# Delta rule on one Trainium2 core: diagonal squares of 16 rows inverted by back substitution on VectorE in place of three doubling levels

## The chip, the cores and the metric

The kernel runs on 1 core of one Trainium2 chip. The metric is device time in microseconds of one execution. TensorE (PE in the rows, with PEld for its weight loads), VectorE (DVE), ScalarE (ACT) and GpSimd (POOL) each run their own instructions in a fixed order; SyncE (SP) issues the DMAs of the kernel before.

## The reference, cut to what matters

Two layers of a hybrid decoder over 256 tokens and 1024 channels. Each layer projects the hidden state, mixes the tokens in three ways (gated DeltaNet, Mamba-2 SSD, MLA attention), merges the three and runs a feed-forward part: dense in layer 0, 8 experts in layer 1. The change lies in the DeltaNet:

```
ia  = eye(C) + where(strict_lower, beta[:, None] * kk * decay, 0)
rhs = concat([v * beta, k * (beta * exp(G))])
sol = triangular_solve(ia, rhs, lower=True, unit_diagonal=True)
...
v_new = u - w @ state
o     = q_dec @ state + qk @ v_new
```

`kk` holds the products of all keys, `decay` their decays, and `ia` is unit lower triangular, so the solve is a product with its inverse. There are 4 heads of 128 channels.

## The kernel before, in words

The kernel works in 2 chunks of 128 tokens (index `t`, `NT` = 2), with the 4 heads side by side in 512 columns of one tile. In `gdn()` it makes, for each `t`, the strictly lower part `N[t]` (line 1062: VectorE reads the product of the keys from PSUM) and then the inverse of identity plus `N[t]`, held in `Sm[t]`.

The inverse is built by doubling. Lines 1075 to 1078 write the inverse of the squares of 2 rows (a product with a mask and a subtraction from the identity, both of 512 columns on VectorE). The loop `lv` from 1 to 6 (line 1087) then doubles the side of the inverted squares from 2 to 128 rows. One level is, for both `t`: 8 products `N` by `Tm` on TensorE (line 1098, tile `smt`), a masked copy into `M1` on VectorE (line 1101, 256 columns; GpSimd clears the rest of `M1`, line 1100), 8 products `M1` by `Sm` (line 1108), a subtraction into `Sm` on VectorE (line 1109) and, up to level 5, 8 transposes of `Sm` (`turn`, line 1073) that ScalarE copies into `Tm`. All products with `Sm`, `Tm`, `N` and `M1` are in plain f32; a trace shows each of them as two passes through TensorE, and a transpose as one.

What fills TensorE meanwhile: every weight comes as a raw f32 tile of 1 MB by DMA, ScalarE rounds it into `whi` (line 170) and VectorE takes the remainder `wlo` (line 172), 128x1024 at a time through a ring of four, and each product is done as three products of rounded halves. `ada_step` (line 199) spreads the conditioning vectors over the same time, one VectorE instruction of 128x1024 after another.

The order of the work: `gdn()`, `ssd()` and a list of fill steps (three convolutions, gates, branch products) are generators. `weave` (line 521) takes one step of `gdn`, one of `ssd` and one of the fill in turn, and `yield` marks where a step ends. Within what that order allows, the framework's scheduler sets the order on each engine when the program is built. Each engine then works strictly in that order.

Of the kernel before, what the change touches and what calls it, by code (L numbers as in the profile page):

```python
# [10 lines left out]
F32 = mybir.dt.float32  # L11
# [3 lines left out]
AF = mybir.ActivationFunctionType  # L15
# [4 lines left out]
P = 128  # L20
# [41 lines left out]
def trunk_kernel(ctx, tc, a, out, dbg=None):  # L62
# [32 lines left out]
    def mm(o, l, r, start, stop):  # L95
        return T.matmul(o, l, r, start=start, stop=stop, skip_group_check=True)  # L96
# [88 lines left out]
    def smtile():  # L185
        return pp.tile([P, 512], F32, name="smt", tag="sm", bufs=3)
# [346 lines left out]
    def mixer(l, after=None):  # L533

        with tc.tile_pool(name=f"mx{l}", bufs=1, reuse_waits="tile") as mp, \
# [3 lines left out]
            def wg(name, dt=F32):  # L539
                return mp.tile([P, 512], dt, name=name, tag="w2k", bufs=16)  # L540
# [469 lines left out]
            def gdn():  # L1010
# [52 lines left out]
                                               op0=OP.mult, op1=OP.mult)  # L1063
                yield

                Sm = [wg("Sm") for _ in range(NT)]
                Tm = [wg("Tm") for _ in range(NT)]
                idb = ident.unsqueeze(1).to_broadcast([P, 4, P])

                def turn(t):  # L1070
                    ps = trtile()
                    for h in range(4):
                        T.transpose(ps[:, hsl[h]], Sm[t][:, hsl[h]], ident)  # L1073
                    A.activation(Tm[t], ps, AF.Copy)
                for t in range(NT):
                    tmp = wg("tmp")
                    V.tensor_mul(h4(tmp), h4(N[t]), cst[:, C_LT0:C_LT0 + P].unsqueeze(1).to_broadcast([P, 4, P]))
                    V.tensor_sub(h4(Sm[t]), idb, h4(tmp))
                qr = raw_rows(0)
                yield  # L1080
                qn = normed(0, *qr)
                yield
                for t in range(NT):
                    turn(t)
                qT = [turned(qn[t]) for t in range(NT)]
                yield
                for lv in range(1, 7):
                    b = 1 << lv
                    lo_ = lambda x: x.rearrange("p (m two b) -> p m two b", two=2, b=b)[:, :, 1]
                    up_ = lambda x: x.rearrange("p (m two b) -> p m two b", two=2, b=b)[:, :, 0]  # L1090
                    v = lambda x: x.rearrange("p (m b) -> p m b", b=b)
                    mk = cst[:, C_LVL + 64 * lv - 64:C_LVL + 64 * lv].rearrange("p (m b) -> p m b", b=b)
                    mk = mk.unsqueeze(1).to_broadcast([P, 4, 64 // b, b])
                    M1s = []
                    for t in range(NT):
                        ps = smtile()
                        for h in range(4):
                            mm(ps[:, h * 64:(h + 1) * 64], N[t][:, hsl[h]], up_(Tm[t][:, hsl[h]]), True, True)
                        M1 = wg("M1")
                        G.memset(lo_(M1), 0.0)  # L1100
                        V.tensor_mul(M1.rearrange("p (h m two b) -> p h m two b", h=4, two=2, b=b)[:, :, :, 0],
                                     ps[:, :256].rearrange("p (h m b) -> p h m b", h=4, b=b), mk)
                        M1s.append(M1)
                    yield
                    for t in range(NT):
                        ps2 = smtile()
                        for h in range(4):
                            mm(ps2[:, h * 64:(h + 1) * 64], M1s[t][:, hsl[h]], lo_(Sm[t][:, hsl[h]]), True, True)
                        V.tensor_sub(lo_(Sm[t]), lo_(Sm[t]), v(ps2[:, :256]))
                    yield  # L1110
                    if lv < 6:
                        for t in range(NT):
                            turn(t)
                    if lv == 2:
                        for t in range(NT):
                            At.append(wg("At"))
                            ps = smtile()
                            for h in range(4):
                                mm(ps[:, hsl[h]], kT[t][:, hsl[h]], qT[t][:, hsl[h]], True, True)
                            V.tensor_mul(At[t], ps, E[t])  # L1120
                    if lv == 3:
                        while fill.has("v"):
                            yield
                        for t in range(NT):
                            psv = trtile()
                            for h in range(4):
                                T.transpose(psv[:, hsl[h]], vc[h][:, t * P:(t + 1) * P], ident)
                            vt.append(wg("vt"))
                            A.activation(vt[t], psv, AF.Copy)
                    if lv < 6:  # L1130
                        yield
                og = []
# [663 lines left out]
```

## Time and profile before

| | us |
|---|---|
| median of 3 runs | 1904.64 (1902.97 to 1906.03) |
| the profiled execution | 1905.8 |
| its span in the trace | 1904.0 |
| TensorE busy | 1847.7 (97%) |
| VectorE busy | 1598.7 (84%) |
| ScalarE busy | 1230.9 (65%) |
| GpSimd busy | 41.5 (2%) |

The token mixing of layer 0 runs until about 322 us, the dense feed-forward part until about 560, the mixing of layer 1 until about 860, and the experts take the rest. `N` is written at 149 us in layer 0 and at 647 us in layer 1; the six levels that follow end at 244 us in layer 0. A busy share is the time that an engine spends inside instructions. For TensorE it says little on how near to its peak it is, since a matmul that is pipelined behind another counts with its whole length. The distance from one start to the next tells what an instruction costs; for TensorE it is read from the weight loads.

### The profile page before, as it was taken

The page shows a single profiled execution, that of the slowest core. Times are in us where ns is not written, and L with a number is a line of the kernel's source. Part 1 is how long each engine was busy: PE and PEld are TensorE (multiplying, and loading weights), DVE is VectorE, ACT ScalarE, POOL GpSimd, SP SyncE. Part 2 cuts the span into 40 slices and gives each one's busy share as a digit, 9 for nine tenths or more (in the row PEclk, how much of TensorE's full clock was granted, in tenths as well). Part 3 has the DMA queues.
Part 4 walks back from the last instruction along what each step waited for, and adds up shares of the span by engine and source line. Part 5 has one row for each costly group of instructions (what it writes and reads, how often), then busy time and mean ns, then how long its engine had stood idle before and what let it go on. Part 6 is the DMA issues. An engine that isn't in the chain of part 4 may idle for free.

```text
span 1904.0 us, 25647 instructions
## 1 busy us (share of the span) xinstructions
PE 1847.7 (97%) x9490; PEld 1548.6 (81%) x9490; DVE 1598.7 (84%) x2313; ACT 1230.9 (65%) x1599; POOL 41.5 (2%) x61
## 2 busy tenths in 40 slices
PE   8989999999999999999999999999999999999996
PEld 6889888788879898888888777878878888788785
DVE  7988786876578987667999889998898999899997
ACT  4655445544455644446777787777777777777775
POOL 0000100000000000000000000000000000000001
PEclk9999999999999999999999999999999999999998
DMA  9463545676545555558899989999889999899892
GB/s 364 175 213 125 199 177 202 241 290 238 205 169 199 198 185 193 176 200 329 334 356 343 354 320 361 343 365 355 339 333 356 351 358 368 311 354 381 332 353 91
DMA packets 75016, 530.19 MB, mean 278 GB/s; under 512 B 8578, under 2 KB 8962, under 8 KB 12548
## 3 DMA queue, kind: packets, MB, share of 16 engines
q1 hardware_dynamic: 74884, 528.49, 73.6%
q8 instruction: 76, 1.25, 0.3%
q14 instruction: 56, 0.46, 0.1%
HBM read 527.41 MB, written 1.05 MB: 278 GB/s over the span
## 4 chain that ended last, share of the span: by engine, by line
PE 84%; DVE 8%; ACT 4%; DMA 2%; issue 2%; ACTq 0%; DVEq 0%; SPq 0%
PE mmt L96 74%; PE smt L96 5%; DVE wlo L172 2%; DMA raw<-in_w_in_dram 2%; PE sst L96 2%; PE trt L1566 1%; DVE raw L199 1%; ACT whi L170 1%; DVE cv L588 1%; ACT sg L1527 1%; PE trt L258 0%; PE trt L1073 0%; PE trt L96 0%; DMA raw<-in_ffn_w_up_dram 0%; ACT htmp L289 0%
## 5 line engine op out<-in xcount | busy, mean ns | idle before, releaser
L172 DVE TENSOR_TENSOR wlo<-raw,whi 128x1024 fp32r<-128x1024 f32 (+1 forms) x874 | 1041.9, 1221 | 151.7 <-ACT whi L170 131.6
L170 ACT ACTIVATE whi<-raw 128x1024 fp32r<-128x1024 f32 (+1 forms) x874 | 907.8, 1059 | 316.4 <-PE mmt L96 263.4
L96 PE MATMUL mmt<-whi,xx 128*128 128x512 f32 x1792 | 578.9, 397 | 0.0
L96 PEld LDWEIGHTS mmt<-whi,xx 128*128 128x128 f32 x1792 | 337.4, 188 | 74.9
L96 PE MATMUL mmt<-wlo,xx 128*128 128x512 f32 x896 | 357.6, 399 | 4.9 <-DVE wlo L172 4.9
L96 PE MATMUL mmt<-whi,act 128*128 128x512 f32 x896 | 281.0, 391 | 1.2 <-ACT whi L170 1.2
L96 PEld LDWEIGHTS mmt<-wlo,xx 128*128 128x128 f32 x896 | 168.8, 188 | 52.1 <-DVE wlo L172 16.5
L96 PEld LDWEIGHTS mmt<-whi,act 128*128 128x128 f32 x896 | 167.4, 188 | 36.4 <-ACT whi L170 2.5
L96 PE MATMUL mmt<-whi,hh 128*128 128x512 f32 (+2 forms) x480 | 183.9, 389 | 4.8 <-ACT hh L292 2.0
L96 PE MATMUL mmt<-wlo,hh 128*128 128x512 f32 (+2 forms) x480 | 180.9, 382 | 1.0 <-DVE wlo L172 1.0
L96 PE MATMUL mmt<-whi,hl 128*128 128x512 f32 (+2 forms) x480 | 180.8, 382 | 0.5 <-DVE hl L293 0.5
L96 PE MATMUL mmt<-wlo,act 128*128 128x512 f32 x448 | 175.2, 391 | 1.8 <-DVE wlo L172 1.6
L199 DVE CUSTOM_DVE_ANT_0 raw<-raw,sc_b,pv 128x1024 f32<-128x1024 f32 x96 | 121.7, 1281 | 7.9 <-DMA raw<-in_w_ada_gate_dram 4.7
L96 PEld LDWEIGHTS mmt<-whi,hh 128*128 128x128 f32 x480 | 90.7, 189 | 22.8 <-ACT hh L292 2.6
L96 PEld LDWEIGHTS mmt<-whi,hl 128*128 128x128 f32 x480 | 90.6, 189 | 18.0 <-DVE hl L293 1.0
L96 PEld LDWEIGHTS mmt<-wlo,hh 128*128 128x128 f32 x480 | 90.6, 189 | 17.4 <-DVE wlo L172 1.6
L96 PEld LDWEIGHTS mmt<-wlo,act 128*128 128x128 f32 x448 | 84.1, 188 | 22.3 <-DVE wlo L172 4.4
L96 PE MATMUL mmt<-hh,wlo 128*128 128x256 f32 x320 | 92.9, 292 | 4.4 <-DVE wlo L172 4.4
L96 PE MATMUL mmt<-hh,whi 128*128 128x256 f32 x320 | 93.4, 293 | 1.5 <-ACT whi L170 1.5
L96 PE MATMUL mmt<-hl,whi 128*128 128x256 f32 x320 | 92.1, 289 | 0.0
L1549 ACT ACTIVATE act<-trt 128x512 fp32r<-128x512 f32 x56 | 33.1, 591 | 72.0 <-PE trt L1566 72.0
L96 PEld LDWEIGHTS mmt<-hh,wlo 128*128 128x128 f32 x320 | 61.9, 194 | 6.0 <-DVE wlo L172 5.8
(422 smaller groups left out, 2209.6 us busy)
## 6 DMA issues: line engine op xcount, KB each, us to landing
raw<-in_moe_w_gate_dram SPq DMA_DIRECT2D x112, 1024.0 KB, 5.9
raw<-in_moe_w_up_dram SPq DMA_DIRECT2D x112, 1024.0 KB, 6.4
raw<-in_moe_w_down_dram SPq DMA_DIRECT2D x112, 1024.0 KB, 6.6
raw<-in_w_in_dram SPq DMA_DIRECT2D x50, 1024.0 KB, 4.9
raw<-in_w_ada_pair_dram SPq DMA_DIRECT2D x32, 1024.0 KB, 5.5
raw<-in_w_ada_gate_dram SPq DMA_DIRECT2D x16, 1024.0 KB, 4.9
raw<-in_ffn_w_down_dram SPq DMA_DIRECT2D x11, 1024.0 KB, 4.8
raw<-in_ffn_w_gate_dram SPq DMA_DIRECT2D x10, 1024.0 KB, 4.9
```

Of the source, the lines that this page charges most:

```text
L96: return T.matmul(o, l, r, start=start, stop=stop, skip_group_check=True)
L170: last["hi"] = A.activation(hi[:, :m], r, AF.Copy)
L172: last["lo"] = V.tensor_sub(lo[:, :m], r, hi[:, :m].bitcast(F32))
L199: last["ada"] = V.tensor_tensor_reduce(r, r, sc_b, 1.0, pv[l][:, PP_BADA + i:PP_BADA + i + 1], OP.mult, OP.add, modc[l][:, i:i + 1])
L588: V.scalar_tensor_tensor(cv[:, s:], o[:, :S - s], tapw(3 - s), cv[:, s:], op0=OP.mult, op1=OP.add)
L1527: A.activation(tmp[:, o], ps[:, o], AF.Identity, scale=sc, bias=sh)
L1549: return trace(*args, **kw)
L1566: last["tr"] = T.transpose(ps[:, b * P:(b + 1) * P], sg[:, b * P:(b + 1) * P], ident)
```

## The change

The levels 1 to 3 and the start with squares of 2 rows go. In their place the 64 diagonal squares of 16 rows (8 squares in each chunk, 2 chunks, 4 heads) are inverted at once, each in one partition of VectorE:

- GpSimd writes both `N[t]` (256 KB each) to a buffer in HBM, `blk_in`, and reads the 64 squares back into `B`, one partition each, by four DMAs of 16 squares, in pieces of 64 bytes. It clears `X` and sets its diagonal to one.
- VectorE changes the sign of `B` (64x256) and does 15 pairs of a product of n by n and a sum over rows of n, n from 1 to 15. Each pair needs the one ahead of it.
- GpSimd writes the 64 inverted squares into a second buffer, `blk_out`, by four DMAs, and loads both `Sm[t]` (256 KB each) from it. What lies outside the squares in `blk_out` is zero; it is cleared once, in layer 0 behind the first products, by a memset on GpSimd and three DMAs of 525 KB together.
- The products `At` and the transposes `vt`, which stood in levels 2 and 3, come behind the back substitution, then `turn`, then the levels 4 to 6 as before.

```diff
+BROW = 16 * 512 + 16
...
+    blk_in = dp.tile([NT * 8, BROW], F32, name="blk_in")
+    blk_out = dp.tile([NT * 8, BROW], F32, name="blk_out")
+    blk_rows = lambda x, t: x[8 * t:8 * t + 8].rearrange("m c -> (m c)")[:P * 512].rearrange("(p c) -> p c", c=512)
+    blk_diag = lambda x, h: x[:, :16 * 512].rearrange("m (j c) -> m j c", j=16)[:, :, h * P:h * P + 16]
...
+                zero = wg("zero")
+                G.memset(zero, 0.0)
+                to = blk_out.rearrange("m c -> (m c)").rearrange("(p c) -> p c", p=P)
+                w = NT * 8 * BROW // P
+                for c in range(0, w, 512):
+                    n = min(512, w - c)
+                    nc.gpsimd.dma_start(to[:, c:c + n], zero[:, :n])
...
+                blk = lambda name: wm(name)[:64, :256].rearrange("p (j i) -> p j i", j=16)
+                B, X = blk("B"), blk("X")
+                for t in range(NT):
+                    nc.gpsimd.dma_start(blk_rows(blk_in, t), N[t])
+                for h in range(4):
+                    nc.gpsimd.dma_start(B[16 * h:16 * h + 16], blk_diag(blk_in, h))
+                x_flat = X.rearrange("p j i -> p (j i)")
+                G.memset(x_flat, 0.0)
+                G.memset(x_flat[:, ::17], 1.0)
...
-                for t in range(NT):
-                    tmp = wg("tmp")
-                    V.tensor_mul(h4(tmp), h4(N[t]), cst[:, C_LT0:C_LT0 + P].unsqueeze(1).to_broadcast([P, 4, P]))
-                    V.tensor_sub(h4(Sm[t]), idb, h4(tmp))
                 qr = raw_rows(0)
                 yield
                 qn = normed(0, *qr)
                 yield
+                V.tensor_scalar(B, B, -1.0, None, op0=OP.mult)
+                prod = wm("prod")
+                for j in range(14, -1, -1):
+                    n = 15 - j
+                    pr = prod[:64, :n * n].rearrange("p (i k) -> p i k", i=n)
+                    V.tensor_tensor(pr, B[:, j, j + 1:].unsqueeze(1).to_broadcast([64, n, n]),
+                                    X[:, j + 1:, j + 1:].rearrange("p k i -> p i k"), op=OP.mult)
+                    V.tensor_reduce(X[:, j, j + 1:], pr, axis=AX.X, op=OP.add)
+                for h in range(4):
+                    nc.gpsimd.dma_start(blk_diag(blk_out, h), X[16 * h:16 * h + 16])
+                for t in range(NT):
+                    nc.gpsimd.dma_start(Sm[t], blk_rows(blk_out, t))
...
-                for lv in range(1, 7):
+                for lv in range(4, 7):
```

How the change moves the instructions is shown at three places. The first is VectorE in layer 0 from the writing of `N` on (`cv` are convolutions, `raw,modc` conditioning, `sq` and `rsq` the norm of the queries). Before:

```order
L1062 SCALAR_TENSOR_TENSOR N<-smt,beta,E 128x128 x8
L1077 TENSOR_TENSOR tmp<-N,cst 128x512
L588 SCALAR_TENSOR_TENSOR cv<-mmt,pv_68,cv 128x254
L1078 TENSOR_TENSOR Sm<-cst,tmp 128x512
L1077 TENSOR_TENSOR tmp<-N,cst 128x512
L588 SCALAR_TENSOR_TENSOR cv<-mmt,pv_68,cv 128x253
L1078 TENSOR_TENSOR Sm<-cst,tmp 128x512
L588 SCALAR_TENSOR_TENSOR cv<-mmt,pv_68,cv 128x255
L172 TENSOR_TENSOR wlo<-raw,whi 128x1024
```

and with the change, from one line behind the `N` rows up to the first sum:

```order
L596 SCALAR_TENSOR_TENSOR cv<-mmt,pv_72,cv 128x253
L1041 TENSOR_REDUCE sq_1548<-sq 128x4 x2
L1103 TENSOR_SCALAR B<-B 64x256
L136 TENSOR_SCALAR rsq_d_1647<-sq_1548 128x8
L596 SCALAR_TENSOR_TENSOR cv<-mmt,pv_72,cv 128x255
L120 TENSOR_SCALAR rsq_y_1649<-rsq_d_1647 128x8
L123 TENSOR_SCALAR rsq_h_1651<-rsq_d_1647 128x8
L1108 TENSOR_TENSOR prod<-B,X 64x1
L129 TENSOR_TENSOR rsq_t_1653<-rsq_y_1649 128x8
L596 SCALAR_TENSOR_TENSOR cv<-mmt,pv_72,cv 128x254
L130 TENSOR_TENSOR rsq_t_1653<-rsq_t_1653,rsq_h_1651 128x8
L1110 TENSOR_REDUCE X<-prod 64x1
```

The row that changes the sign of `B` stands only some dozen instructions behind `N`, and everything below it on VectorE, the `wlo` of the weights among it, waits until `B` has come back from HBM.

The second place is GpSimd in layer 0 behind `kd`. With the change:

```order
L1068 TENSOR_TENSOR kd<-nrm,kde 128x512
L1085 DMA blk_in<-N 128x512 x2
L1087 DMA B<-blk_in 16x16x16 x4
L1089 MEMSET X 64x256
L1090 MEMSET X 64x16
L1112 DMA blk_out<-X 16x16x16 x4
L1114 DMA Sm<-blk_out 128x512 x2
L1149 MEMSET M_1942 128x16x16
L1149 MEMSET M_1950 128x16x16
```

Before, the memsets of `M1` followed `kd` directly. Now twelve DMAs in two legs, out and back each, stand in GpSimd's order ahead of them.

The third place is TensorE in layer 0 around the first `turn` (`trt<-cst,Sm`). With the change:

```order
L104 MATMUL smt<-xT 128x128 x8
L1129 MATMUL trt<-cst,cv 128x128 x8
L1097 MATMUL trt<-cst,Sm 128x128 x4
L104 MATMUL mmt<-whi,hh 128x512
L1097 MATMUL trt<-cst,Sm 128x128 x4
L104 MATMUL mmt<-wlo,hh 128x512
L104 MATMUL mmt<-whi,hl 128x512
L104 MATMUL smt<-Tm,N 128x64 x8
L104 MATMUL mmt<-whi,hh 128x512
L104 MATMUL mmt<-wlo,hh 128x512
L104 MATMUL smt<-Sm,M_1942 128x64 x4
L104 MATMUL smt<-Sm,M_1950 128x64 x4
```

The first of these transposes waits for the load of `Sm[0]` from HBM, and the fill products (`mmt`) behind it wait with it. `At` (the first row) and `vt` (the second) now stand ahead of it; before, they stood between the levels.

## Rows read from the trace of the kernel before

**Rows 1.** The page's busy times: each engine's busy us, its share of the span, and its instructions.

```profile
PE 1847.7 (97%) x9490; PEld 1548.6 (81%) x9490; DVE 1598.7 (84%) x2313; ACT 1230.9 (65%) x1599; POOL 41.5 (2%) x61
```

**Rows 2.** The table by windows, layer 0: the window and its length, busy us and instructions of PE, PEld, DVE, ACT and POOL, then the granted TensorE clock, the DMA share and GB/s.

```profile
140.00:150.00 10.00, 9.95 (x85) 9.75 (x84) 10.00 (x26) 6.15 (x12) 2.48 (x1) 1.00 0.47 158
150.00:160.00 10.00, 10.00 (x87) 9.82 (x86) 9.91 (x24) 6.75 (x13) 0.34 (x1) 1.00 0.42 151
160.00:170.00 10.00, 10.00 (x85) 9.76 (x85) 8.97 (x25) 5.44 (x11) 0.65 (x2) 1.00 0.33 117
170.00:180.00 10.00, 9.98 (x87) 9.76 (x87) 6.75 (x15) 2.58 (x5) 0.63 (x2) 1.00 0.29 105
```

**Rows 3.** The timeline of TensorE in layer 0, level 3: start, us, engine, line, operation, tiles.

```profile
149.09 1.05 PE L96 MATMUL smt<-xT 128*128 128x128 f32 x8
...
185.47 1.90 PE L96 MATMUL smt<-Tm,N 128*128 128x64 f32 x16
...
190.70 1.89 PE L96 MATMUL smt<-Sm,M 128*128 128x64 f32 x16
...
195.94 1.03 PE L1073 MATMUL trt<-cst,Sm 128*128 128x128 f32 x8
```

**Rows 4.** The same, layer 1: the last products ahead of `N`, up to the first instruction behind them.

```profile
644.80 1.73 PE L96 MATMUL smt<-xT 128*128 128x128 f32 x14
646.36 0.60 PE L1022 MATMUL trt<-cst,cv 128*128 128x128 f32 x4
```

**Rows 5.** The timeline of VectorE in both layers: one row for each kind of instruction that the sum uses.

```profile
142.40 0.47 DVE L588 SCALAR_TENSOR_TENSOR cv<-mmt,pv,cv 128x255 f32<-128x255 f32 x1
142.79 0.15 DVE L123 SCALAR_TENSOR_TENSOR rsq_y<-rsq_t,rsq_y 128x8 f32<-128x8 f32 x1
142.87 0.47 DVE L588 SCALAR_TENSOR_TENSOR cv<-mmt,pv,cv 128x254 f32<-128x254 f32 x1
...
148.98 2.33 DVE L1062 SCALAR_TENSOR_TENSOR N<-smt,beta,E 128x128 f32<-128x128 f32 x8
151.22 0.68 DVE L1077 TENSOR_TENSOR tmp<-N,cst 128x512 f32<-128x512 f32 x1
151.82 0.48 DVE L588 SCALAR_TENSOR_TENSOR cv<-mmt,pv,cv 128x254 f32<-128x254 f32 x1
...
170.58 0.43 DVE L1101 TENSOR_TENSOR M<-smt,cst 128x256 f32<-128x256 f32 x1 [0.47 <-PE smt L96]
170.92 0.47 DVE L588 SCALAR_TENSOR_TENSOR cv<-mmt,pv,cv 128x253 f32<-128x253 f32 x1
...
194.17 2.36 DVE L172 TENSOR_TENSOR wlo<-raw,whi 128x1024 fp32r<-128x1024 f32 x2
196.45 1.28 DVE L199 CUSTOM_DVE_ANT_0 raw<-raw,sc_b,pv 128x1024 f32<-128x1024 f32 x1
197.65 0.08 DVE L199 DVE_READ_ACCUMULATOR2_ANT modc<- 128x1 f32 x1
...
646.64 2.15 DVE L1062 SCALAR_TENSOR_TENSOR N<-smt,beta,E 128x128 f32<-128x128 f32 x8
648.71 0.67 DVE L1077 TENSOR_TENSOR tmp<-N,cst 128x512 f32<-128x512 f32 x1
...
661.77 0.17 DVE L121 TENSOR_TENSOR rsq_t<-rsq_y 128x8 f32<-128x8 f32 x1
661.97 0.17 DVE L122 TENSOR_TENSOR rsq_t<-rsq_t,rsq_h 128x8 f32<-128x8 f32 x1
```

**Rows 6.** What TensorE's weight loads waited for from 560 to 860 us (mixing of layer 1): the one that waits, what it waited for, us in total, times, the longest.

```profile
PEld mmt L96 <- DVE wlo L172: 2.6, 4, 1.4
```

**Rows 7.** The page's DMA issues: tiles, queue, count, KB each, median us from issue to landing; and two rows of SP's own timeline with the time that an issue takes there.

```profile
raw<-in_w_in_dram SPq DMA_DIRECT2D x50, 1024.0 KB, 4.9
raw<-in_mla_w_uk_dram SPq DMA_DIRECT2D x2, 512.0 KB, 3.5
out_dram<-raw SPq DMA_DIRECT2D x4, 256.0 KB, 2.7
...
2.30 0.43 SPq L1672 DMA_DIRECT2D cst<-in_consts_dram  x1
190.54 0.33 SPq L148 DMA_DIRECT2D raw<-in_w_ada_pair_dram  x1
```

**Rows 8.** The timeline of GpSimd: its instruction `kd` in layer 0 and in layer 1; and VectorE's row that starts during the first.

```profile
145.49 2.48 POOL L1053 TENSOR_TENSOR kd<-nrm,kde 128x512 f32<-128x512 f32 x1 [80.77 <-DVE nrm L1037]
643.08 1.35 POOL L1053 TENSOR_TENSOR kd<-nrm,kde 128x512 f32<-128x512 f32 x1 [75.95 <-DVE nrm L1037]
...
147.39 1.67 DVE L172 TENSOR_TENSOR wlo<-raw,whi 128x1024 fp32r<-128x1024 f32 x1
```

**Rows 9.** The timeline of the weight loads around two waits in layer 0, and the table by windows there (columns as in rows 2).

```profile
118.25 0.19 PEld L96 LDWEIGHTS mmt<-hh,whi 128*128 128x128 f32 x1
118.38 0.19 PEld L96 LDWEIGHTS mmt<-hl,whi 128*128 128x128 f32 x1
120.84 0.42 PEld L812 LDWEIGHTS trt<-cst,sc 128*128 128x128 f32 x4 [2.27 <-issue]
123.30 0.29 PEld L96 LDWEIGHTS mmt<-hh,wlo 128*128 128x128 f32 x1 [2.04 <-DVE wlo L172]
...
124.00:126.00 2.00, 2.00 (x11) 2.00 (x11) 2.00 (x5) 1.91 (x6) 0.00 (x0) 0.50 0.80 225
126.00:128.00 2.00, 2.00 (x12) 2.00 (x11) 1.96 (x5) 0.47 (x1) 0.00 (x0) 0.50 0.71 299
130.00:132.00 2.00, 2.00 (x20) 2.00 (x19) 0.72 (x2) 1.07 (x4) 0.00 (x0) 1.00 0.98 418
```

**Rows 10.** The table by windows at the start of the kernel (columns as in rows 2).

```profile
20.00:30.00 10.00, 10.00 (x48) 8.47 (x48) 8.53 (x13) 3.68 (x6) 0.00 (x0) 1.00 1.01 413
```

**Rows 11.** The timeline of the weight loads, products of 512 columns, layer 0.

```profile
183.15 0.19 PEld L96 LDWEIGHTS mmt<-whi,hh 128*128 128x128 f32 x1
183.38 0.19 PEld L96 LDWEIGHTS mmt<-wlo,hh 128*128 128x128 f32 x1
```

More of the change, by code (lines that the diff above doesn't have):

```diff
@@ L72, in trunk_kernel @@
     V.memset(ones, 1.0)
+    dp = ctx.enter_context(tc.tile_pool(name="dp", bufs=1, space=bass.MemoryType.DRAM))
+    blk_in = dp.tile([NT * 8, BROW], F32, name="blk_in")
+    blk_out = dp.tile([NT * 8, BROW], F32, name="blk_out")
+    blk_rows = lambda x, t: x[8 * t:8 * t + 8].rearrange("m c -> (m c)")[:P * 512].rearrange("(p c) -> p c", c=512)
+    blk_diag = lambda x, h: x[:, :16 * 512].rearrange("m (j c) -> m j c", j=16)[:, :, h * P:h * P + 16]
     xs = cp.tile([P, NT, D], F32, name="xs")
@@ L1064, in gdn @@
                 yield
+                blk = lambda name: wm(name)[:64, :256].rearrange("p (j i) -> p j i", j=16)
[7 more added lines that the diff above has]
+                G.memset(x_flat[:, ::17], 1.0)
                 Sm = [wg("Sm") for _ in range(NT)]
                 Tm = [wg("Tm") for _ in range(NT)]
-                idb = ident.unsqueeze(1).to_broadcast([P, 4, P])
                 def turn(t):
@@ L1082, in gdn @@
                 yield
+                V.tensor_scalar(B, B, -1.0, None, op0=OP.mult)
[10 more added lines that the diff above has]
+                    nc.gpsimd.dma_start(Sm[t], blk_rows(blk_out, t))
+                qT = [turned(qn[t]) for t in range(NT)]
+                yield
+                for t in range(NT):
+                    At.append(wg("At"))
+                    ps = smtile()
+                    for h in range(4):
+                        mm(ps[:, hsl[h]], kT[t][:, hsl[h]], qT[t][:, hsl[h]], True, True)
+                    V.tensor_mul(At[t], ps, E[t])
+                yield
+                while fill.has("v"):
+                    yield
+                for t in range(NT):
+                    psv = trtile()
+                    for h in range(4):
+                        T.transpose(psv[:, hsl[h]], vc[h][:, t * P:(t + 1) * P], ident)
+                    vt.append(wg("vt"))
+                    A.activation(vt[t], psv, AF.Copy)
+                yield
                 for t in range(NT):
                     turn(t)
-                qT = [turned(qn[t]) for t in range(NT)]
                 yield
-                for lv in range(1, 7):
+                for lv in range(4, 7):
                     b = 1 << lv
@@ L1113, in gdn @@
                             turn(t)
[L1114 to L1129, printed above, removed]
                     if lv < 6:
```

## The prediction

> **What bounds the kernel now.** The page's busy times come first: TensorE is busy for 97% of the span [rows 1], so time is gained only where TensorE has less to do, and only if nothing else makes it wait there. Since pipelined matmuls count with their whole length, the table by windows of the stretch that changes comes next [rows 2]: from 150 to 180 us TensorE starts 85 to 87 matmuls in each 10 us, one per 0.117 us, at full clock and without a gap. TensorE is truly the bound there. The reader is to see in the same rows that VectorE has no slack either: 10.00 and 9.91 of 10 us from 140 to 160. The two engines are balanced, so work taken from TensorE alone uncovers VectorE. The table of waits for layer 1 says the same: weight loads already wait 2.6 us for `wlo` there [rows 6].
>
> A change worth less than 0.2%, or 3.8 us, can't be told from none here. The sum is made against the profiled execution, 1905.8 us (its span is 1904.0); the median of the runs is 1.2 below that, 1904.64.
>
> **TensorE: what goes.** A level costs 1.90 us for the 16 passes of `N` by `Tm`, 1.89 for the 16 of `M1` by `Sm`, and 1.03 for the 8 transposes [rows 3]: 4.82. Three levels in two layers are 28.9 us, and nothing is added on TensorE. `At`, `vt` and the first `turn` are moved, not changed. ScalarE's copies and GpSimd's memsets of the three levels are beside the path.
>
> **VectorE: about even.** Distances between starts [rows 5] are 0.60 us for 512 columns (tmp, 151.22 to 151.82), 0.075 for 8, 0.34 for 256 out of PSUM (170.58 to 170.92), 0.39 for a row of a convolution, 1.13 for a `wlo`, 1.20 for a conditioning row. Removed per layer: 4 of 512 (2.4) and 12 of 256 (4.1). Added: the lines through these rows give about 0.067 + n/960 us for n columns; the 15 pairs have 1240 columns twice, so 2 x (15 x 0.067 + 1.29) = 4.6, and 0.3 for the sign: 4.9. That is 1.6 less than what goes.
>
> **What TensorE meets instead.** I tally both engines in the new order, from the last `N` to the `wlo` that stands in front of the last sum.
> - Layer 0: VectorE has 7 `wlo` (7.9), 3 conditioning (3.6), 26 convolution rows (10.1), 7 of 512 (4.2), 13 small (1.0) and the solve without its last sum (4.6): 31.4 us. TensorE, up to the product that needs this `wlo`, has 132 of 256 columns (15.7 at 0.119), 34 of 512 (7.8 at 0.23 [rows 11]), 24 transposes (2.9), 14 products in f32 of two passes (3.3) and 0.4: 30.1. VectorE ends `N` 1.3 us behind TensorE's last product for it (149.9, the eighth of eight in 1.05 us, against 151.2 [rows 3, 5]). TensorE so waits 1.3 + 1.3 = 2.6 us.
> - Layer 1: 10 `wlo` (11.3), 6 conditioning (7.2), 15 convolution rows (5.9), 4.2, 1.0 and 4.6 are 34.2 us, against 192 of 256 (22.8), 30 of 512 (6.9), 24 transposes (2.9) and 0.2: 32.8. `N` ends 2.4 us behind (646.3 against 648.7 [rows 4, 5]): 3.8 us, of which 2.6 [rows 6] are waited now already: 1.2.
> - A pair whose neighbour in the order is only an 8-column row shows its latency: dependent small rows start 0.20 us apart, not 0.075 (661.77 to 661.97) [rows 5]. About 6 of the 30 steps stand so: 0.7 us a layer.
>
> **The two legs through HBM.** No row of before shows a DMA issued by GpSimd or one in pieces of 64 bytes, so each leg is bounded. Out: `N` is written, and only when both have landed are four reads of `B` issued: behind the last `N` there are 5 issues and 2 landings. Back: 4 writes of `X`, a landing, the load of `Sm[0]`, a landing: the same. Low end: 0.33 us an issue and 2.7 a landing [rows 7] give 5 x 0.33 + 2 x 2.7 = 7.05 us. High end: 1.35 an issue (GpSimd's own `kd` undisturbed [rows 8]) and 4.9 a landing (1 MB [rows 7]) give 16.6. I take 0.7 an issue, twice SP's, since what GpSimd has to do for one is not shown, and 3.6 a landing, nearest to the 3.5 of 512 KB, which both `N` together are: a leg of 10.7 us.
> - Out: VectorE reaches the sign of `B` after 7.8 us (2 x 1.20, 2 x 1.13, 2 x 0.60, 5 x 0.39) in layer 0 and 7.1 in layer 1. It waits 2.9 and 3.6, and every `wlo` behind it is late by as much.
> - Back: in layer 0 the solve ends 31.7 us of rows behind `N`, TensorE reaches `turn` after 38.9. From TensorE's side the solve ends at 1.3 + 31.7 = 33.0 and `turn` at 38.9 + 2.6 = 41.5, with the waits that both share left out: 8.5 of the leg are covered, 2.2 not. In layer 1 it is 2.4 + 34.5 = 36.9 against 39.4 + 3.8 = 43.2: 6.3 covered, 4.4 not.
>
> The Trainium skill (DMA: Bandwidth & Descriptors, section on the anatomy of one DMA on the gpsimd path) gives a fixed cost of some 2.0 us per DMA plus its bytes at 436 GB/s; by that both legs would be covered, an estimate that puts the result near 1883. The trace's 2.7 for 256 KB [rows 7] agrees on SP's queue, and no row shows GpSimd's.
>
> **Two smaller terms.** Clearing `blk_out`: 525 KB at 413 GB/s are 1.3 us; its tile is a fresh buffer, so the DMAs go out at the very start, where the DMA share is 1.01 [rows 10]. I charge 1.4; below, it is free if TensorE's products set the pace there. The clock: after two waits of 2.3 and 2.0 us the granted clock was 0.50, 1.2 GHz [rows 9], with 23 loads in 4 us where 20 go in 2 at full clock: 1.7 us lost. I charge it once, for the 4.4 us ahead of `turn` in layer 1. When TensorE slows at the other waits, VectorE is the later of the two and nothing is lost.
>
> **The sum.** Layer 0 waits 2.6 + 2.9 + 0.7 + 2.2 = 8.4, layer 1 1.2 + 3.6 + 0.7 + 4.4 = 9.9. So 28.9 - 18.3 - 1.4 - 1.7 = 7.5 us are gained: 1905.8 becomes 1898.3, and the median 1897.1. For a leg of L us the gain is 52.0 - 4L less the clock's share: each microsecond of a leg costs four, at two places in each of two layers.
>
> **The rivals.**
> - *The legs are hidden.* At 7.05 us a leg only the balance of the engines is left: 3.3 us in layer 0, 2.7 in layer 1, the clearing 1.4; the gain is 21.5, and the time 1883. For it: the 2.7 us of the page, and a DMA share of 0.3 to 0.5 in this stretch [rows 2]. Against it: four issues in a row by software, and tiny pieces.
> - *Slower: GpSimd's DMAs are held up by VectorE.* In layer 0 `kd` took 2.48 us, in layer 1 1.35, and the `wlo` beside it 1.67 in place of 1.22 [rows 5, 8]: the two engines block each other, 1.13 us at a time, in one case of two. If every issue pays half of that, an issue takes 1.27 and a leg 13.5 us: 52.0 - 54.0 - 3.4 (the clock falls at both `turn`) = -5.4, or 1910. It decides from a leg of 13.1 us on. The Trainium skill (SBUF — State Buffer, section on the two separate sides) warns of exactly this: while VectorE holds the port pair that it shares with GpSimd, GpSimd can't write descriptors; by that rule alone, with VectorE busy without a break here, this rival holds. The blocked `kd` agrees that there is a lock; no row shows it for descriptors.
> - *No change: the solve is a chain.* If all 30 steps show their 0.12 us of latency, the solve costs 3.6 in place of 0.7 a layer, 5.8 in all: 1903. Against it: the order puts a convolution row or a `wlo` between most steps. A leg of 11.6 to 13.1 us comes out as no change too.
>
> **How the numbers follow.** My forecast gets 0.36, the hidden legs 0.22, no change 0.17, slower 0.25. So faster is 0.58, same 0.17, slower 0.25. The range starts with the hidden legs and a free clearing (1904.64 - 22.9 = 1882) and takes in the slower rival with a further half microsecond of leg (1912). The long end of 16.6 us (1919 and more) is left out.
>
> **What would show it.** Right: 28 fewer rows on TensorE; the row of `B` waits on a DMA for about 3 us, some 8 us behind `N`; products wait for `wlo` at 170 to 180 us; `turn` waits on the load of `Sm` for 2 us in layer 0 and 4 in layer 1, with a fallen clock behind the latter. Wrong: no wait at `B` (legs under 8 us), or one of over 6; waits of the levels 4 to 6 that I have at zero, since the two chunks take turns there; or a start that is later by more than 1.4 us.

## The result and the profile after

The changed kernel took 1916.1 us (median of 4 runs, 1915.5 to 1923.5), the kernel before 1905.3 beside it: a ratio of 1.0067, interval 1.0046 to 1.0087. Run again later (e9), it took 1914.5 (six runs, 1912.8 to 1922.3) against 1904.9: 1.0055, interval 1.0037 to 1.0072. So it is slower by some 10 us, where 7.5 us of gain were forecast. The profiled execution after is the longest of its four, 1923.5 us (span 1921.5); that of e9, 1915.1 us with a span of 1913.1, lies near the median. Both are read below.

The busy times of the changed kernel, to set beside [rows 1]:

```profile
PE 1841.4 (96%) x9250; PEld 1537.7 (80%) x9250; DVE 1595.8 (83%) x2343; ACT 1225.7 (64%) x1587; POOL 53.8 (3%) x81
```

They hardly say anything: TensorE's busy time fell by 6 us, though three levels went. The table by windows says more, if each window is one whole layer of mixing: from the first row of the rsqrt ahead of `N` to that behind the mixing, in each run at its own times (columns as in [rows 2]). Before:

```profile
138.40:338.70 200.30, 199.47 (x1232) 176.29 (x1231) 156.59 (x313) 100.42 (x164) 16.92 (x20) 1.00 0.49 180
635.80:857.80 222.00, 217.18 (x1291) 189.35 (x1290) 170.10 (x329) 108.20 (x171) 14.71 (x19) 1.00 0.53 190
```

The changed kernel, profiled execution:

```profile
141.00:351.20 210.20, 198.67 (x1111) 172.98 (x1110) 154.03 (x328) 98.12 (x158) 21.22 (x28) 0.94 0.49 178
649.00:874.90 225.90, 210.25 (x1171) 180.92 (x1170) 170.30 (x344) 105.41 (x165) 20.38 (x27) 0.97 0.55 192
```

The changed kernel again (e9):

```profile
139.30:343.30 204.00, 191.20 (x1111) 165.63 (x1111) 154.47 (x328) 97.98 (x158) 21.22 (x28) 0.98 0.50 183
641.90:866.60 224.70, 210.56 (x1171) 181.23 (x1170) 170.34 (x344) 105.45 (x165) 20.34 (x27) 0.97 0.54 193
```

Four of the experiments below, each with its two rows: e3, e4, e12 and e15.

```profile
140.00:332.10 192.10, 187.12 (x1111) 162.88 (x1111) 154.65 (x328) 97.62 (x158) 23.31 (x28) 1.00 0.54 195
629.50:846.40 216.90, 206.24 (x1171) 177.85 (x1171) 169.46 (x345) 105.12 (x165) 19.92 (x27) 0.98 0.56 200
...
137.70:325.70 188.00, 186.49 (x1111) 163.34 (x1110) 153.57 (x328) 97.33 (x158) 17.50 (x22) 1.00 0.55 198
629.80:841.60 211.80, 203.90 (x1171) 175.70 (x1171) 169.64 (x344) 104.43 (x165) 17.27 (x21) 1.00 0.57 204
...
137.50:330.50 193.00, 188.99 (x1111) 163.92 (x1110) 154.00 (x328) 97.94 (x158) 15.10 (x16) 0.99 0.54 194
627.90:846.40 218.50, 209.18 (x1171) 178.20 (x1170) 171.00 (x345) 105.15 (x165) 13.51 (x15) 0.98 0.56 198
...
138.30:330.90 192.60, 191.12 (x1151) 167.12 (x1151) 151.68 (x316) 98.53 (x160) 14.88 (x18) 1.00 0.55 194
629.10:844.20 215.10, 209.68 (x1211) 180.58 (x1211) 168.09 (x333) 105.88 (x167) 13.63 (x17) 1.00 0.57 201
```

Each row splits its length into three. Idle is the length less TensorE's busy time. Lost to the clock is the length times what the granted clock lacks to 1.00 (two digits, so within 1 us); half clock that falls into a pause is counted there too, so this term is at the high end and the rest at the low one. The rest is work at full clock.

| us: rest + idle + clock | layer 0 | layer 1 |
|---|---|---|
| before | 199.5 + 0.8 + 0 = 200.3 | 217.2 + 4.8 + 0 = 222.0 |
| change, profiled | 186.1 + 11.5 + 12.6 = 210.2 | 203.5 + 15.6 + 6.8 = 225.9 |
| change again (e9) | 187.1 + 12.8 + 4.1 = 204.0 | 203.8 + 14.1 + 6.7 = 224.7 |
| no back leg (e3) | 187.1 + 5.0 + 0 = 192.1 | 201.9 + 10.7 + 4.3 = 216.9 |
| no legs (e4) | 186.5 + 1.5 + 0 = 188.0 | 203.9 + 7.9 + 0 = 211.8 |
| legs on SyncE (e12) | 187.1 + 4.0 + 1.9 = 193.0 | 204.8 + 9.3 + 4.4 = 218.5 |
| SyncE, squares of 8 (e15) | 191.1 + 1.5 + 0 = 192.6 | 209.7 + 5.4 + 0 = 215.1 |

The reader is to see that the rest is nearly the same in every run with squares of 16 rows (within 1 us in layer 0, 3 in layer 1), and 12 to 15 us a layer below before: the work did go. Idle time and clock took it back.

The legs, in GpSimd's timeline of layer 0 (profiled execution; the 3.38 us put down to TensorE are the landing of `N`, as e9 has it at the same place):

```profile
152.96 0.62 POOL L1085 DMA_DIRECT2D blk_in<-N  x1 [2.42 <-DVE N L1077]
154.17 0.54 POOL L1085 DMA_DIRECT2D blk_in<-N  x1 [0.60 <-DVE N L1077]
158.09 2.28 POOL L1087 DMA_DIRECT2D B<-blk_in  x4 [3.38 <-PE smt L104]
189.89 2.23 POOL L1112 DMA_DIRECT2D blk_out<-X  x4 [29.02 <-DVE X L1110]
198.57 1.14 POOL L1114 DMA_DIRECT2D Sm<-blk_out  x2 [6.45 <-DMA blk_out<-X]
```

VectorE's rows of `B` in both layers, and the last row of the solve:

```profile
164.60 0.28 DVE L1103 TENSOR_SCALAR B<-B 64x256 f32<-64x256 f32 x1 [1.61 <-DMA B<-blk_in]
188.92 0.37 DVE L1110 TENSOR_REDUCE X<-prod 64x15 f32<-64x225 f32 x1
675.02 0.28 DVE L1103 TENSOR_SCALAR B<-B 64x256 f32<-64x256 f32 x1 [5.77 <-DMA B<-blk_in]
704.71 0.38 DVE L1110 TENSOR_REDUCE X<-prod 64x15 f32<-64x225 f32 x1
```

TensorE's longest waits:

```profile
204.55 0.87 PE L1097 MATMUL trt<-cst,Sm 128*128 128x128 f32 x3 [4.94 <-DMA Sm<-blk_out]
676.86 0.58 PE L104 MATMUL mmt<-hh,wlo 128*128 128x256 f32 x1 [4.70 <-DVE wlo L180]
710.94 0.73 PE L104 MATMUL mmt<-whi,hh 128*128 128x512 f32 x2 [2.02 <-ACT whi L178]
```

`X` is ready at 189.3 and the turn starts at 204.55: the back leg of layer 0 took 15.3 us. In layer 1 the turn waits for nothing, but VectorE stands 5.8 us for `B`, and a product waits 4.7 for the `wlo` behind it.

### The profile page after: what moved, and what is told of

The parts are those of the page before. It is cut to its first block, busy times and chain, and to the rows that moved or that the text cites. A ratio compares the mean times of both kernels' runs of the same rounds, so it can differ in the third digit from the quotient of the medians.

```text
span 1921.5 us, 25250 instructions
## 1 busy us (share of the span) xinstructions
PE 1841.4 (96%) x9250; PEld 1537.7 (80%) x9250; DVE 1595.8 (83%) x2343; ACT 1225.7 (64%) x1587; POOL 53.8 (3%) x81
## 4 chain that ended last, share of the span: by engine, by line
PE 77%; DVE 12%; DMA 4%; ACT 4%; issue 2%; POOL 0%; SPq 0%; DVEq 0%; ACTq 0%; POOLq 0%
PE mmt L104 69%; PE smt L104 4%; DVE wlo L180 3%; DVE raw L207 2%; DVE cv L596 1%; PE sst L104 1%; PE trt L1599 1%; ACT whi L178 1%; DMA raw<-in_w_in_dram 1%; DMA B<-blk_in 1%; ACT sg L1560 1%; DMA pv<-in_params_dram 0%; PE trt L266 0%; DMA raw<-in_ffn_w_gate_dram 0%; PE trt L104 0%
## 5 line engine op out<-in xcount | busy, mean ns | idle before, releaser
L207 DVE CUSTOM_DVE_ANT_0 raw<-raw,sc_b,pv 128x1024 f32<-128x1024 f32 x96 | 121.3, 1278 | 11.2 <-DMA raw<-in_w_ada_pair_dram 5.7
L104 PEld LDWEIGHTS mmt<-hh,wlo 128*128 128x128 f32 x320 | 64.0, 201 | 10.8 <-DVE wlo L180 10.7
```

What stands on the lines that cost most here:

```text
L207: last["ada"] = V.tensor_tensor_reduce(r, r, sc_b, 1.0, pv[l][:, PP_BADA + i:PP_BADA + i + 1], OP.mult, OP.add, modc[l][:, i:i + 1])
```

## The experiments

Times are medians of 4 to 12 runs each, with 13 to 17 of before (1904.8 to 1905.2) beside them; "the change" is 1916.1, or 1914.5 in e9. Line numbers are those of the changed kernel.

**e9, the change again.** No edit.

> The changed kernel itself once more, as the base for the others: its first four runs lie at 1915.5 to 1916.3 and one at 1923.5. Expected: a median of 1915 to 1918.

Measured: 1914.5. The base is good to some 2 us, and single executions scatter by 9.

**e1, cleared late.**

```diff
                 G.memset(zero, 0.0)
+                zero = cp.tile([P, 128], F32, name="zl")
+                with tc.issue_after(last["late"].ins):
+                    G.memset(zero, 0.0)
...
-                for c in range(0, w, 512):
+                for c in range(0, w, 128):
...
```

`last["late"]` is GpSimd's instruction on the late parameters; the clearing goes out in nine DMAs in place of three.

> The changed kernel with one edit: blk_out is cleared by GpSimd behind its work on the late parameters (some 56 us into the run), not at the start; the order of every other engine is the same. Theory A (the clearing takes DMA time from the first loads: xs[1] arrives 3.3 us later on VectorE than before): the first rows stand where they stood before the change, and the time falls by 3.3 us, 1916.1 to about 1912.8. Rival (the late first loads are hidden behind later waits of the same stage, or the shift comes from something else): the rows ahead of 40 us stay late, or the time stays within 1 us of 1916.

Measured: 1912.5, ratio 1.0040 (1.0025 to 1.0056); 1.9 to 3.6 us less than the change. The first row of the rsqrt on VectorE stands at 8.19 us, as before (8.20); in the change it stood at 11.47. Theory A holds.

**e2 to e4, the legs taken out.** e2 has the first edit, e3 the second, e4 both and the late clearing.

```diff
-                    nc.gpsimd.dma_start(B[16 * h:16 * h + 16], blk_diag(blk_in, h))
+                    nc.gpsimd.dma_start(B[16 * h:16 * h + 16], blk_diag(blk_out, h))
...
-                    nc.gpsimd.dma_start(Sm[t], blk_rows(blk_out, t))
+                    nc.gpsimd.dma_start(Sm[t], blk_rows(blk_in, t))
```

> The changed kernel, but the four reads of B come from blk_out, which nobody writes at that time, in place of blk_in, so that VectorE waits for no landing ahead of the sign of B (the values solved are not those of N). Theory A (waits for the legs, and the clock behind them): the 5.8 us wait in front of B in layer 1 and the 1.6 us in layer 0 go, with them TensorE's 4.7 us for wlo and some 3 us of the half clock behind it: 6 to 9 us less, 1907 to 1910. Theory B (the legs are covered, and what costs is VectorE's solve, its 30 small rows and the order around it): under 2 us less, 1914 or more.

> The changed kernel, but Sm is loaded from blk_in, once N is written there, in place of blk_out, so that the turn waits for no X (the levels 4 to 6 work on other values). Theory A: in layer 0 TensorE's 4.9 us in front of the turn go, and the half clock from 203.6 to 221 us behind it with them (18 us at half clock in the profiled run, less in the others); in layer 1 nothing waits there. 5 us for the wait and 4 to 8 for the clock: 1903 to 1907. Theory B: under 2 us less, 1914 or more.

> All three edits together: late clearing, B from blk_out, Sm from blk_in; as many DMAs as in the changed kernel, the same solve on VectorE, but no wait of an engine for a round trip through HBM. Theory A: what is left of the change is 28.9 us of TensorE less the balance of the engines (2.6 and 1.2 us) and the solve's own latency (1.4): 1882 to 1890. Theory B: the solve and the uncovered levels hold the time at 1905 or more.

Measured: e2 1910.4 (ratio 1.0028, 1.0017 to 1.0039), e3 1897.5 (0.9961, 0.9949 to 0.9974), e4 1884.3 (0.9885, 0.9871 to 0.9899). Theory A holds for e4 and, within half a microsecond, for e2; e3 goes beyond it. Against the change (both bases) the out leg costs 4 to 6 us, the back leg 17 to 19, all together 30 to 32. Theory B falls: with the same 30 rows on VectorE and no wait for DMA the change gains 20.7 us. In e3 the work's order moves too (the turn stands 27 us earlier), so its price is that of the leg and of what the order does for it. In e2 and e4 VectorE changes the sign of `B` before `N` is written (142.2 us against 150.4 in e2), so the solve waits for `N` no longer: their prices hold that as well.

**e5, TensorE kept busy through the wait.**

```diff
+                if l == 0:
+                    ps = trtile()
+                    for _ in range(44):
+                        T.transpose(ps[:, :P], ident, ident)
                 for t in range(NT):
                     turn(t)
```

> The changed kernel with 44 transposes of the identity on TensorE (some 4.9 us at full clock, read by nobody) directly in front of the turn of layer 0, where TensorE stands idle for 4.9 us. Theory A (the clock falls because TensorE stands idle there): the granted clock stays at 1.00 behind the turn, and the 18 us at half clock of layer 0 go; the time falls by 4 to 8 us, to 1908 to 1912, although work was added. Rival (the clock falls with the kind of work that follows, the small f32 products of the levels): the half clock stays, and the time rises by up to 4.9 us, 1916 to 1921.

Measured: 1914.0, 0.5 to 2.1 less than the change. The table by windows, 4 us each, right behind the turn of layer 0 says why. The change, profiled:

```profile
204.00:208.00 4.00, 3.45 (x14) 3.10 (x15) 0.00 (x0) 1.65 (x4) 0.00 (x0) 0.50 0.59 236
212.00:216.00 4.00, 4.00 (x19) 3.80 (x18) 1.18 (x4) 0.00 (x0) 0.62 (x2) 0.50 0.00 0
```

The change again (e9), where the turn waited for 4.79 us:

```profile
204.00:208.00 4.00, 3.77 (x20) 3.48 (x20) 0.00 (x0) 1.96 (x5) 0.00 (x0) 0.63 0.53 207
212.00:216.00 4.00, 3.93 (x33) 3.57 (x32) 2.94 (x6) 1.08 (x2) 0.00 (x0) 1.00 0.22 33
```

e5:

```profile
204.00:208.00 4.00, 3.40 (x30) 3.15 (x29) 2.27 (x5) 1.19 (x2) 0.30 (x2) 1.00 0.81 266
212.00:216.00 4.00, 4.00 (x36) 3.88 (x35) 1.69 (x4) 0.00 (x0) 0.31 (x1) 1.00 0.00 0
```

With TensorE busy the clock stays at 1.00 through the same levels, and in e9 it is back at 1.00 while they run, so it is the standing still that lowers it and the rival falls. The time misses theory A's 1908 to 1912. The transposes take the place of the wait, and the wait of e9 cost only some 3 us at 1.2 GHz; the profiled execution of the change stayed there to some 223 us. Which of the two is the usual length is open: e1, e2, e8 and e10 lose 6.8 to 8.5 us in the one spell around the turn of layer 0, e6 1.7 as e9 does.

**e6 and e7, one layer alone.** `gdn()` takes the old doubling in the other layer; `blk_out` is cleared in both.

```diff
+                if l == 0:   # e7: l == 1
...                          # the solve, levels 4 to 6 behind it
+                else:
...                          # levels 0 to 6 as before the change
```

> The solve in layer 0 only; layer 1 starts its doubling at level 1 as before the change. From the two profiles layer 0 costs 3.3 us at the start and 9.9 us in the mixer, of which about 7 are clock that the other runs of the changed kernel did not all pay; layer 1 costs 3.9. By these sums: 1910 to 1913. If the loss is the same in both layers (one common cause on VectorE): about 1911.5 here and 1908 with the solve in layer 1 only (the start counts here, and there as well).

> The solve in layer 1 only; the clearing of blk_out at the start stays. From the two profiles: 3.3 us for the start and 3.9 for layer 1: 1912 to 1913. Rival (layer 1's loss is mostly the 4.7 us wait for wlo, which another order of the loads in another run may not have): down to 1907.

Measured: 1916.8 and 1910.9. Layer 0 alone costs as much as the change, layer 1 alone 6 us; less the clearing, the two add up to more than both together. Neither expectation on the split holds for e6, whose profile has 4.3 us of its loss between the two mixings (301.4 us for 297.1), where nothing was changed; e7 lies between its expectation and the rival. They only say that layer 0 is the dearer one.

**e8, four more turns of the weave ahead of the turn.** Four more `yield` lines ahead of `turn(t)`.

> The changed kernel with four more turns of the weave ahead of the turn, so that more products of the fill stand between the solve and the wait for Sm. Theory A: in layer 0 the 4.9 us wait and the half clock behind it go, at no work added: 1905 to 1911. Against it: the fill that is brought forward lacks behind, where the levels 4 to 6 then stand with nothing between their steps; if that is worth as much, the time stays at 1914 to 1918.

Measured: 1916.0. TensorE still waits 4.23 us at the turn: more fill ahead of it did not stand between `X` and the turn. Theory A misses.

**e10, one landing less.** Sm is loaded from `blk_in`, issued behind the DMAs of `X` but not behind their landing.

```diff
-                    nc.gpsimd.dma_start(blk_diag(blk_out, h), X[16 * h:16 * h + 16])
...
-                    nc.gpsimd.dma_start(Sm[t], blk_rows(blk_out, t))
+                    last["x"] = nc.gpsimd.dma_start(blk_diag(blk_out, h), X[16 * h:16 * h + 16])
...
+                    with tc.issue_after(last["x"].ins):
+                        nc.gpsimd.dma_start(Sm[t], blk_rows(blk_in, t))
```

> The changed kernel, but Sm is loaded from blk_in by DMAs that GpSimd issues behind those of X without waiting for their landing (the levels work on other values): the back leg has its 6 issues and one landing, in place of two. It was 15.3 us in layer 0 (last row of X ends at 189.2, the load of Sm lands at 204.5), 6.5 of them in the wait for the landing of X. Theory A (the leg's length behind the solve is what costs, past a cover of some 10 us): with 8.8 us left it is covered, and most of the 18.6 us of the back leg come back: 1899 to 1904. Rival (half the landings, half the cost): 1906 to 1909. Rival (what costs is that the turn depends on X at all, since X itself is late): 1912 or more.

Measured: 1915.6 (1.0054, 1.0041 to 1.0067). Theory A misses, and the rows show that the leg was not cut as far as the edit says:

```profile
200.85 1.09 PE L1097 MATMUL trt<-cst,Sm 128*128 128x128 f32 x4 [2.26 <-DMA Sm<-blk_in]
203.07 1.09 PE L1097 MATMUL trt<-cst,Sm 128*128 128x128 f32 x4 [1.14 <-DMA Sm<-blk_in]
```

`X` ends at 190.3; the second `Sm` is there at 203.07, 12.8 us later and not 8.8; that both transfers now run beside each other and the weight loads is the likely reason, not a shown one. The waits of the two turns are 3.4 us in place of 4.8, and in its profile the clock stays low to 217 us behind them.

**e11, squares of 8 rows.** `BROW = 8 * 512 + 8`, 128 partitions of 64 numbers, 7 pairs, `range(3, 7)`; late clearing.

> The change with squares of 8 rows: 128 partitions, 7 pairs of at most 49 columns in place of 15 of up to 225, and doubling from level 3; clearing late as in e1. TensorE gets back one level in two layers (9.6 us), VectorE loses 3.2 us of pairs a layer and gets 1.3 back, and X is ready 14 to 16 rows of other work earlier, some 10 us. Theory A (the back leg's cost is X's lateness plus the leg, 18.6 us by e3): most of that goes against 9.6 us of work: 1912.5 - 18.6 + 9.6 - 4 = 1900, between 1897 and 1905. Rival (the out leg and the four pieces of the chain that stay hold it): 1908 to 1915.

Measured: 1907.3 (1.0012, 0.9996 to 1.0027). Between the two expectations: `X` is ready some 12 us (layer 0) and 16 us (layer 1) sooner behind `N` than in e1, but VectorE waits 3.6 and 6.7 us for `B`, and the turn of layer 1 now waits 2.8 for `Sm`.

**e12, e13, the legs in other queues**, with the late clearing. e12 has `nc.sync`, e13 `nc.scalar`, at four lines:

```diff
-                    nc.gpsimd.dma_start(blk_rows(blk_in, t), N[t])
+                    nc.sync.dma_start(blk_rows(blk_in, t), N[t])
```

> The change with the DMAs of both legs issued by SyncE, in its queue with the weight loads, in place of GpSimd; clearing late as in e1. An issue takes 0.33 us there in place of 0.57 (six of them in the back leg: 1.4 us less), and the weight loads behind them wait, so that the pieces of 64 bytes meet less traffic (their landing took 6.4 us beside loads, 3.8 without). Theory A: the back leg falls from 15.3 to some 10 us and out by 1 to 3: 1900 to 1907. Rival (SyncE's queue is held up at the waits for N and X, and the weight loads come late for the product chain): 1912 to 1920.

> As e12, but ScalarE issues both legs, in its own order: not in software, not in the queue of the weight loads. If GpSimd's software issue made the legs long: they are as short as in e12 (back leg some 9 us in layer 0) and the time is near 1895 plus what ScalarE's own waits cost. If the weight loads beside them did: pieces of 64 bytes still land after 5 to 7 us where loads run, the back leg of layer 0 stays at 12 us or more, and the time lies at 1902 to 1912.

Measured: e12 1895.2 (0.9951, 0.9939 to 0.9964), faster than both kernels and below theory A's range; e13 1917.6 (1.0057, 1.0040 to 1.0075), above both of its ranges. The back leg of layer 0, from the last row of `X` to `Sm`, is 15.1 us in e9, 13.2 in e13 and some 9.6 in e12 (its last issue ends at 193.7, plus a landing of 2.7). SyncE's queue shows what differs. In the change again it holds weight loads alone, five of 1 MB while the leg runs:

```profile
188.89 0.33 SPq L156 DMA_DIRECT2D raw<-in_w_ada_pair_dram  x1
190.35 0.33 SPq L156 DMA_DIRECT2D raw<-in_w_in_dram  x1
192.62 0.33 SPq L156 DMA_DIRECT2D raw<-in_w_branch_c_dram  x1
196.78 0.33 SPq L156 DMA_DIRECT2D raw<-in_w_ada_pair_dram  x1
201.88 0.33 SPq L156 DMA_DIRECT2D raw<-in_w_branch_c_dram  x1
```

In e12 a load that comes up while the leg runs is issued behind what of the leg is already there: after two loads at 183.5 and 185.0 us, one of 1 MB stands between the two halves of the leg and the next behind it:

```profile
186.90 2.18 SPq L1115 DMA_DIRECT2D blk_out<-X  x4
189.19 0.39 SPq L156 DMA_DIRECT2D raw<-in_w_branch_c_dram  x1
192.90 0.81 SPq L1117 DMA_DIRECT2D Sm<-blk_out  x2
193.81 0.38 SPq L156 DMA_DIRECT2D raw<-in_w_ada_pair_dram  x1
```

The issue in software is the smaller part: e13's issues take 0.33 to 0.48 us (medians), and its leg stays long. That the loads from another queue stretch the legs is argued from these rows, since no run has the legs in GpSimd's queue without loads (the 3.8 us in the expectation of e12 were not without: SyncE issued loads at 704.9 and some 708.7 us beside them). It agrees with the Trainium skill (DMA: Bandwidth & Descriptors, section on queues, rings and completion order): each DMA engine takes turns between the queues that have work. e13 pays on top that ScalarE itself stands 2.3 us ahead of `sq` and 2.1 ahead of `xT`, where its own DMAs wait for a landing. e12 gains by order too: its turn stands at 203.2, 16 us behind `X`, where the change reaches it 10 us behind. On the way out, VectorE waits for `B` in neither layer, where it stood 5.8 us in layer 1 of the change. How much of the 17 us from e1 to e12 is the legs and how much the order is not told apart.

**e14, the solve traced ahead of the rows of `q`**, otherwise e12.

> As e12, with the solve traced ahead of the rows of q, so that VectorE takes its steps before that other work where both are ready. If X's lateness still costs after e12: X is ready sooner, the turn comes sooner, and more fill is left between the levels: 1886 to 1893. If e12's legs are covered already: within 3 us of 1895, or slower, since q and with it At come later.

Measured: 1901.4 (0.9985, 0.9976 to 0.9993), 6 more than e12. That fits the second expectation, but does not show that the legs were covered: the edit did not bring `X` sooner in layer 0 (38.1 us behind `N`, 36.5 in e12), and in both layers the turn comes later behind `N`, by 13 and by 10 us, in layer 1 although `X` is 9.5 us sooner. TensorE waits 2.9 us in layer 0 for a row of the rsqrt on VectorE and 2.9 in layer 1 for ScalarE, which e12 does not have; which moved row is behind it was not followed up.

**e15, squares of 8 with the legs on SyncE**, e11 and e12 together.

> As e12, with squares of 8 rows: 14 steps of the solve in place of 30, and level 3 on TensorE again. If e12's legs are covered, the level's 9.6 us come back as loss, less 1.9 us of VectorE a layer where it is the later engine: 1899 to 1905. If X's lateness still costs 10 us: 1889 to 1895.

Measured: 1891.5 (0.9924, 0.9911 to 0.9937), the fastest of those that leave nothing out. The level it does again on TensorE costs 4 to 5 us a layer in the table's first term; idle and clock give back 4.4 and 8.3. So e12 was not fully covered: the second expectation holds, and e14 could not show it.

## Why the prediction was wrong

The forecast was 7.5 us of gain, the range ended at 1912, and the kernel came out slower. The step that failed is what a wait for the legs costs: the clock behind it, charged once (point 4), and on the back leg the waits in other places than the turn (point 3). By the profile of e9 against that of before the spans differ by +9.1, so 16.6 us are missing. Point by point:

1. **TensorE's work** was to fall by 14.45 us a layer. It fell by 12.4 and 13.4: 3.1 missing. (TensorE has 240 instructions less, 9490 to 9250 [rows 1], not the 28 that one of the signs named.)
2. **VectorE even**: right. Without legs (e4) the idle time grows by 0.7 and 3.1 us; 3.3 and 1.9 were forecast.
3. **The legs** were taken as 10.7 us each. The out leg of layer 0 took 10.7 (153.9 to 164.6), that of layer 1 13.1; the back leg of layer 0 15.3. The waits came elsewhere than foretold (5.8 at `B` in layer 1 for 3.6; 4.9 at the turn of layer 0 for 2.2; none at that of layer 1 for 4.4). Idle time grew by 12.0 and 9.3, 21.3 in all, where 18.3 stood in the sum: 3.0 missing. Taken out one by one, the out leg gave 4 to 6 us (e2), where 2.9 + 3.6 were charged, and the back leg 17 to 19 (e3), where 2.2 + 4.4 and the clock's 1.7 were. So the sum is short on the back leg. From e9 to e3 idle time falls by 11.2 us and the clock term by 6.5; only 4.8 of the 11.2 stood at the turn. The rest are waits for `wlo`, `whi` and `cv` ahead of it, in a stretch where the change has no levels to run and e3, whose turn stands 27 us earlier, has them. The tally had one such wait in each layer.
4. **The clock** is the largest term that failed. I charged 1.7 us once and wrote that at the other waits VectorE is the later engine "and nothing is lost". The rows say otherwise: 4.1 + 6.7 = 10.8 us in e9, 19.4 in the profiled execution. In e9 it falls behind four of the five pauses of more than 2 us, those too that are no wait for a leg, and once, at 186 us, behind shorter ones. Layer 1 of e9, TensorE's waits:

```profile
669.86 0.58 PE L104 MATMUL mmt<-hh,wlo 128*128 128x256 f32 x1 [4.57 <-DVE wlo L180]
687.06 0.33 PE L961 MATMUL sst<-cst,cv 128*128 128x128 f32 x1 [2.16 <-ACT cv L911]
704.11 0.74 PE L104 MATMUL mmt<-whi,hh 128*128 128x512 f32 x2 [2.16 <-ACT whi L178]
```

and the windows that hold them:

```profile
668.00:672.00 4.00, 2.14 (x10) 2.14 (x11) 3.98 (x15) 1.18 (x2) 0.00 (x0) 0.50 0.06 23
688.00:692.00 4.00, 4.00 (x22) 4.00 (x23) 3.77 (x8) 2.01 (x2) 0.00 (x0) 0.57 0.39 141
704.00:708.00 4.00, 3.19 (x13) 2.76 (x14) 3.09 (x4) 3.34 (x6) 1.40 (x3) 0.66 0.87 313
```

   Each of the two pauses of 2.2 us is followed by some 1.7 us lost. Not every pause is: behind one of 2.15 us in layer 0 of e9 (166.95) and one of 3.70 in layer 1 of e4 (654.88) the clock stayed at 1.00.

```profile
166.95 0.33 PE L961 MATMUL sst<-cst,cv 128*128 128x128 f32 x1 [2.15 <-ACT cv L911]
168.00:172.00 4.00, 2.92 (x21) 2.40 (x21) 4.00 (x17) 1.05 (x3) 0.00 (x0) 1.00 0.22 41
...
654.88 0.39 PE L104 MATMUL mmt<-hh,whi 128*128 128x256 f32 x1 [3.70 <-ACT whi L178]
656.00:660.00 4.00, 3.75 (x34) 3.51 (x32) 3.48 (x9) 3.58 (x5) 0.95 (x3) 1.00 0.61 197
```

   The price of one event was right, its count was not: in windows of 1 us e9 loses 10.2 us, six times 1.7. By the table 9.1 are missing, and 3.1 + 3.0 + 9.1 = 15.2 of the 16.6. Over TensorE's busy time alone the clock takes 3.0 + 5.6 us in e9; then 6.9 are the clock's and 5.4 the work's, with nearly the same sum. That the time would fall by all of it at full clock is not shown: in the windows above VectorE is busy for 3.98, 3.77 and 3.09 of 4 us, so part of it could come back as waiting for VectorE. What the runs do show is that the clock falls because TensorE stands (e5), and that without the legs it does not fall in the mixings (e4).
5. **The clearing** delays the first rows by 3.3 us, not 1.4: one of the signs of being wrong that the prediction named. VectorE's second row of `xs` and first row of the rsqrt, before and after:

```profile
6.30 0.69 DVE L300 CUSTOM_DVE_ANT_0 xn<-xs 128x512 f32<-128x512 f32 x1 [0.63 <-DMA xs<-in_x_dram]
8.20 0.17 DVE L112 TENSOR_SCALAR rsq_y<-ssd 128x2 int32<-128x2 int32 x1
```

```profile
8.90 0.69 DVE L308 CUSTOM_DVE_ANT_0 xn<-xs 128x512 f32<-128x512 f32 x1 [2.53 <-DMA xs<-in_x_dram]
11.47 0.17 DVE L120 TENSOR_SCALAR rsq_y<-ssd 128x2 int32<-128x2 int32 x1
```

   I priced its bytes; it also delays the loads that everything waits for, since its DMAs are issued at 1.6 to 3.4 us, ahead of the first products and not behind them. Not all of the 3.3 us reach the end: outside the two mixings the spans of e9 and before differ by 2.7 us, 1.3 more than was charged, which is nearly all that was left of the 16.6.

The rivals. "GpSimd's DMAs are held up by VectorE" had the right sign and the wrong mechanism: GpSimd issued all its DMAs of the legs at 0.54 to 0.62 us, with VectorE busy beside it, nothing like 1.27. The Trainium skill (SBUF — State Buffer, two separate sides) ties the blocked descriptors to VectorE's 2-port modes and says that a `tensor_tensor` did not stall a DMA; the prediction left that condition out. The rows agree with it, as `wlo`, a `tensor_tensor`, ran beside the issues. "The legs are hidden" gave 1883; e4, where no engine waits for them, took 1884.3. With the clearing free, as in e4, and no wait for a leg the same sum is 28.9 - 3.3 - 1.9 = 23.7 us, and e4 gained 20.7. So the model of the engines held to 3 us, and the fixed cost of 2.0 us per DMA that the Trainium skill states (DMA: Bandwidth & Descriptors, anatomy of one DMA) is what did not: here the DMAs of the legs landed 2.4 to 7.6 us after their issue. "The solve is a chain" did not come: the scheduler put a row of other work between nearly all its steps.

## What to carry to other kernels

Count every place where TensorE will stand, and charge each with the wait and with the half clock that may follow; here idle time grew by 21.3 us and the clock took half as much again. Ask also what work is left to run while a round trip is under way: most of what the back leg cost did not stand at the wait for it. A round trip through HBM beside large loads from another queue cost more than its landing alone: in the queue of those loads the kernel was 17 us faster here, the change of order included. Clearing DMAs behind the first loads saved 2 to 4. And ask which size of the on-chip step is right only when its legs are hidden: squares of 8 were no better than the kernel before in e11, and the best in e15.

## What the runs showed of the hardware

- Two executions of one program, after waits of 4.94 and 4.79 us at the same place, stayed at 1.2 GHz for some 20 and some 3 us. Of the 8.4 us between their spans 6.2 lie in the mixing of layer 0, where their clock terms differ by 8.5. What decides it no run here shows.
- Four DMAs of 16 KB in pieces of 64 bytes (`B`, layer 1) landed after 7.2 us from GpSimd's queue and 8.9 from ScalarE's; the weight loads of 1 MB beside them took 7.3 to 8.9 us (medians), where 4.9 is the median before [rows 7]. From SyncE's queue, between the loads, `B` landed after 5.2 (medians). The DMAs of `X` took 6.4 us from GpSimd in layer 0, with three loads issued within 4 us, and 3.8 in layer 1, with two.
- The same length of pause did and did not lower the clock: in e9 one of 2.16 us in layer 1 (687.06) cost 1.7 us at 1.2 GHz, one of 2.15 us in layer 0 (166.95) nothing.
